# Column means of an 8192 x 8192 matrix: the last rows cut as 4, 4, 2 and 1 blocks, with five blocks loaded early and a small load behind the last

## The chip, the cores and the metric

The kernel runs on one core of one Trainium2 chip. The metric is the device time of one execution in microseconds; the median of three runs of the kernel before is 628.57 us (628.53 to 629.09). The profile covers a span of 626.7 us, from the first to the last instruction.

## The reference

```
x = randn(8192, 8192), float32          # 268.4 MB
out = mean(x, axis=0)                   # 8192 values, float32
```

All of `x` must be read once. A row group is 128 rows of `x`, one for each partition, so there are 64 groups (0 to 63) of 4 MB each. A block is F = 512 columns, so each group has 16 blocks.

## The kernel before

Loads run on SyncE's queue into four row buffers, two groups at a time. VectorE adds the two groups and then adds the sum to `acc`. The last groups come singly, and TensorE adds up what is left, with a matrix of `ones` filled with 1/8192 that also sums over the partitions. TensorE writes four blocks side by side, in four quarters of 32 partitions, which give one 512-column bank of PSUM. ScalarE and VectorE copy PSUM to SBUF, and from there the result is stored.

```python
load(head[:], rows(G - 4)[:, :3 * F])                   # 3 blocks of group 60, first of all
first, second = load_rows(0, 0, 4), load_rows(4, 4, 2)
load(ahead[:], rows(G - 1)[:, 8 * F:WHOLE * F])         # 4 blocks of group 63, early
...
while g < G - 10:                                       # groups 6 to 53, in pairs
    u = (g + 2) % 4
    dma = load_rows(g, u, 2)
    add(both, bufs[:, u, :], bufs[:, u + 1, :], [dma])
    add(acc, acc, both, [])
    g += 2
while g < G - 4:                                        # groups 54 to 59, singly
    row = bufs[:, (g + 2) % 4, :]
    add(acc, acc, row, [load(row, rows(g))])
    g += 1
for lo, loaded in [(3, 3), (5, 0)]:                     # groups 60 and 61
    row = bufs[:, (g + 2) % 4, :]
    dma = load(row[:, loaded * F:], rows(g)[:, loaded * F:])
    add(acc[:, lo * F:], acc[:, lo * F:], row[:, lo * F:], [dma])
    g += 1
...
load(r62, rows(g))                                      # group 62
tc.keep_in_program_order(nc.gpsimd.tensor_add(
    out=acc[:, 13 * F:], in0=acc[:, 13 * F:], in1=r62[:, 13 * F:]))
g += 1
for lo, hi in [(0, 8), (12, 14), (14, 16)]:             # group 63: the last three loads
    load(r63[:, lo * F:hi * F], rows(g)[:, lo * F:hi * F])
# ... matmuls, one for each block or half block, in the order of a plan:
#     ahead, acc, r61, head, acc, r62, acc, r63 0-8, r63 12-14, r63 14-16 ...
copy(res[:, 2, :], banks[2][:])                         # ScalarE
s2 = store(nc.scalar, <blocks 8-12>, res[0:P:32, 2, :], loads[-3])
for b in range(2):
    copy(res[:, b, :], banks[b][:])
copy(tails[0], ends[0][:])
nc.vector.tensor_copy(out=tails[1], in_=ends[1][:])
...
s01 = store(nc.sync, <blocks 0-8>, res[0:P:32, 0:2, :])
s3 = store(nc.scalar, <blocks 12-14>)
store(nc.sync, <blocks 14-16>)
```

The full source:

Of the kernel before, what the change touches and what calls it, by code (L numbers as in the profile page):

```python
# [8 lines left out]
@with_exitstack  # L9
def kernel(  # L10
    ctx: ExitStack,
    tc: tile.TileContext,
    x: bass.AP,
    out: bass.AP,
):

    nc = tc.nc
    f32 = mybir.dt.float32
    M, N = x.shape  # L40
    P = nc.NUM_PARTITIONS
    F = 512
    W = F // 2
    WHOLE = 12
    G = M // P
    U = 6
    sync = mybir.DependencyInfo(mybir.DependencyClass.Sync, mybir.DependencyReason.DATA)

    sb = ctx.enter_context(tc.tile_pool(name="sb", bufs=1))
    psp = ctx.enter_context(tc.tile_pool(name="psum", bufs=1, space=bass.MemoryType.PSUM))  # L50

    bufs = sb.tile([P, U, N], f32, name="bufs")
    both = bufs[:, U - 2, :]
    acc = bufs[:, U - 1, :]
    ones = sb.tile([P, 32], f32, name="ones")
    ahead = sb.tile([P, 4 * F], f32, name="ahead")
    tail = sb.tile([P, W], f32, name="tail")
    warm = sb.tile([P, 32], f32, name="warm")
    nc.gpsimd.memset(ones[:], 1.0 / M)  # L59
    ready = sb.tile([P, 1], f32, name="ready")  # L60
    tc.keep_in_program_order(
        nc.gpsimd.tensor_add(out=ready[:], in0=ones[:, 0:1], in1=ones[:, 1:2]))  # L62
    banks = [psp.tile([P, F], f32, name=f"bank{b}") for b in range(3)]
    ends = [psp.tile([P, W], f32, name=f"end{e}") for e in range(2)]

    loads = []

    def landed(*inss):

        nop = tc.keep_in_program_order(nc.sync.nop()).ins  # L70
        for o in inss:
            tc.add_manual_dep(nop, o.name, sync, reason="SyncE waits")

    def load(dst, src):
        ins = tc.keep_in_program_order(nc.sync.dma_start(out=dst, in_=src)).ins  # L75
        k = len(loads)
        over = loads[k - 8:k - 6] if k >= 8 and k % 2 == 0 else []
        tc.declare_no_dep(ins, group="loads", keep=over, reason="the reader of the buffer waited")
        for o in over:
            tc.add_manual_dep(ins, o.name, sync, reason="covers the next load too")  # L80
        tc.add_to_no_dep_group("loads", ins)
        loads.append(ins)
        return ins

    def rows(g, n=1):
        return x[g * P:(g + n) * P, :]

    def load_rows(g, u, n):
        return load(bufs[:, u:u + n, :], rows(g, n).rearrange("(p j) c -> p j c", j=n))

    adds, joins = [], {}

    def add(dst, a, b, dmas):

        ins = nc.vector.tensor_add(out=dst, in0=a, in1=b).ins  # L95
        if dmas and adds:
            waiter = nc.scalar if len(adds) % 8 > 1 else nc.gpsimd
            nop = joins[waiter] = tc.keep_in_program_order(waiter.nop()).ins  # L98
            for o in dmas + adds[-1:]:
                tc.add_manual_dep(nop, o.name, sync, reason="the no-op waits")  # L100
            for group in ("loads", "adds"):
                tc.declare_no_dep(ins, group=group, reason="the no-op waited")
            tc.add_manual_dep(ins, nop.name, sync, reason="waits for both at once")
        elif adds:
            tc.declare_no_dep(ins, group="loads", reason="the add ahead waited")
        tc.add_to_no_dep_group("adds", ins)
        adds.append(ins)

    head = sb.tile([P, 3 * F], f32, name="head")
    load(head[:], rows(G - 4)[:, :3 * F])  # L110
    first, second = load_rows(0, 0, 4), load_rows(4, 4, 2)
    load(ahead[:], rows(G - 1)[:, 8 * F:WHOLE * F])
    add(bufs[:, 2:4, :], bufs[:, 2:4, :], bufs[:, 0:2, :], [first])
    add(bufs[:, 4:6, :], bufs[:, 4:6, :], bufs[:, 2:4, :], [second])
    add(acc, acc, both, [])
    tc.keep_in_program_order(nc.scalar.copy(out=warm[:], in_=ones[:]))  # L116
    g = 6
    while g < G - 10:
        u = (g + 2) % 4
        dma = load_rows(g, u, 2)  # L120
        add(both, bufs[:, u, :], bufs[:, u + 1, :], [dma])
        add(acc, acc, both, [])
        g += 2

    while g < G - 4:
        row = bufs[:, (g + 2) % 4, :]
        add(acc, acc, row, [load(row, rows(g))])
        g += 1
    for lo, loaded in [(3, 3), (5, 0)]:
        row = bufs[:, (g + 2) % 4, :]  # L130
        dma = load(row[:, loaded * F:], rows(g)[:, loaded * F:])
        add(acc[:, lo * F:], acc[:, lo * F:], row[:, lo * F:], [dma])
        g += 1
    r61, r62, r63 = [bufs[:, (g + 1 + j) % 4, :] for j in range(3)]
    load(r62, rows(g))
    tc.keep_in_program_order(nc.gpsimd.tensor_add(  # L136
        out=acc[:, 13 * F:], in0=acc[:, 13 * F:], in1=r62[:, 13 * F:]))
    g += 1
    for lo, hi in [(0, 8), (12, 14), (14, 16)]:
        load(r63[:, lo * F:hi * F], rows(g)[:, lo * F:hi * F])  # L140

    plan = [
        (ahead, 8, 12),
        (acc, 3, 5),
        (acc, 0, 3),
        (r61, 0, 5),
        (head, 0, 3),
        (acc, 5, 12),
        (r62, 0, 12),
        (r62, 12, 13),  # L150
        (acc, 12, 14),
        (acc, 14, 16),
        (r63, 0, 8),
        (r63, 12, 14),
        (r63, 14, 16),
    ]
    sums = []
    for row, lo, hi in plan:
        base = 8 * F if row is ahead else 0
        if lo < WHOLE:  # L160
            for i in range(lo, hi):
                cols = row[:, i * F - base:(i + 1) * F - base]
                sums.append((banks[i // 4], i % 4, cols))
        else:
            for c in range(lo * F, hi * F, W):
                e, q = divmod(c // W - 2 * WHOLE, 4)
                sums.append((ends[e], q, row[:, c:c + W]))
    for n, (dst, q, cols) in enumerate(sums):
        tc.keep_in_program_order(nc.tensor.matmul(  # L169
            out=dst[32 * q:32 * q + 32, :],  # L170
            lhsT=ones[:],
            rhs=cols,
            start=all(d is not dst or k != q for d, k, _ in sums[:n]),
            stop=all(d is not dst or k != q for d, k, _ in sums[n + 1:]),
            tile_position=(0, 32 * q),
            skip_group_check=True,
        ))

    res = both[:, :3 * F].rearrange("p (b c) -> p b c", b=3)
    tails = [both[:, 3 * F:3 * F + W], tail[:]]  # L180

    def copy(dst, src):
        tc.keep_in_program_order(nc.scalar.copy(out=dst, in_=src))  # L183

    def store(engine, dst, src, *then):
        ins = tc.keep_in_program_order(engine.dma_start(out=dst, in_=src)).ins
        for o in then:
            tc.add_manual_dep(ins, o.name, sync, reason="follows that load")
        return ins

    def end(e):
        return (out[(WHOLE + 2 * e) * F:(WHOLE + 2 * e + 2) * F].rearrange("(q c) -> q c", q=4),
                tails[e][0:P:32, :])

    copy(res[:, 2, :], banks[2][:])
    s2 = store(nc.scalar, out[8 * F:12 * F].rearrange("(q c) -> q c", q=4), res[0:P:32, 2, :],
               loads[-3])
    for b in range(2):
        copy(res[:, b, :], banks[b][:])
    copy(tails[0], ends[0][:])  # L200
    nc.vector.tensor_copy(out=tails[1], in_=ends[1][:])  # L201
    landed(*loads[-8:-6])
    landed(*loads[-6:-4])
    landed(*loads[-4:-2])
    landed(*joins.values())
    s01 = store(nc.sync, out[:8 * F].rearrange("(b q c) -> q b c", b=2, q=4), res[0:P:32, 0:2, :])
    s3 = store(nc.scalar, *end(0))
    store(nc.sync, *end(1))
    landed(loads[-2], s2)
    landed(loads[-1], adds[-1])  # L210
    landed(s01, s3)
    hold = tc.keep_in_program_order(nc.vector.nop()).ins
    tc.add_manual_dep(hold, s01.name, sync, reason="VectorE ends late")


# [28 lines left out]
```

## Time and profile before

| what | value |
|---|---|
| time, median of 3 | 628.57 us |
| span of the profile | 626.7 us |
| VectorE busy | 526.1 us (84%), 60 instructions |
| TensorE, ScalarE, GpSimd busy | 17.6, 3.5 and 4.0 us |
| load queue, share of 16 engines | 99.2% |
| mean rate over the span | 428 GB/s |

The page's forty slices give the busy share of each engine in tenths, and below it that of the 16 transfer engines (DMA). The chain of waits goes back from the last instruction to what released it, and so tells which work the end hung on. The timeline lists instructions by start time, with the idle time ahead of them and what ended it in brackets. A "q" behind an engine's name is its queue of transfer issues; an issue takes some 0.3 to 1.1 us there, and the transfer itself lands later. Group 62 lands near 615.6 us, where GpSimd's add starts.

### The profile page before, as it was taken

To read this page: it belongs to the slowest core of one execution; us is meant where nothing else is said; L and a number is where in the kernel's file an instruction comes from. 1 tells how busy PE (TensorE), PEld (TensorE's weight loads), DVE (VectorE), ACT (ScalarE), POOL (GpSimd) and SP (SyncE) were. 2 spreads that over 40 slices of the span, in tenths; PEclk is the share of its full clock that TensorE was granted. 3 is DMA by queue.
4 is the path that set the end of the run, shared out by engine and by line. 5 is a ranking of instruction groups with operands and counts; after the bars stand their busy time and mean duration, and the time that the engine had idled before them with its cause. 6 is when DMAs were issued, how large, how long until landed. Compare 5 with 4: busy or idle time off the path is not lost.

```text
span 626.7 us, 475 instructions
## 1 busy us (share of the span) xinstructions
PE 17.6 (3%) x124; PEld 5.1 (1%) x124; DVE 526.1 (84%) x60; ACT 3.5 (1%) x6; POOL 4.0 (1%) x7
## 2 busy tenths in 40 slices
PE   0000100000000000000000000000000000000027
PEld 0000000000000000000000000000000000000002
DVE  0028999999888998888988889888898888999991
ACT  0000000000000000000000000000000000000001
POOL 0000000000000000000000000000000000000002
PEclk9999999999999999999999999999999999999999
DMA  9999999999999999999999999999999999999997
GB/s 385 468 402 409 461 443 427 410 460 406 464 402 468 402 468 402 468 402 468 402 468 402 468 402 468 402 460 410 443 427 414 456 402 435 435 435 435 420 433 305
DMA packets 5926, 268.50 MB, mean 428 GB/s; under 512 B 656, under 2 KB 664, under 8 KB 1060
## 3 DMA queue, kind: packets, MB, share of 16 engines
q1 hardware_dynamic: 5908, 268.46, 99.2%
q8 instruction: 1, 0.02, 0.0%
q10 hardware_dynamic: 16, 0.01, 0.0%
q14 instruction: 1, 0.01, 0.0%
HBM read 268.44 MB, written 0.03 MB: 428 GB/s over the span
## 4 chain that ended last, share of the span: by engine, by line
DMA 56%; DVE 33%; another core or an unknown queue 10%; issue 0%; SPq 0%; PE 0%; ACTq 0%; POOLq 0%; POOL 0%
DMA bufs<-in_x_dram 56%; DVE bufs L95 33%; SPq L75 0%; PE end L169 0%; ACTq L98 0%; DVE tail L201 0%; POOLq L98 0%; POOL ready L62 0%; POOL ones L59 0%; POOLq L228 0%
## 5 line engine op out<-in xcount | busy, mean ns | idle before, releaser
L95 DVE TENSOR_TENSOR bufs<-bufs 128x8192 f32<-128x8192 f32 (+3 forms) x59 | 525.6, 8909 | 87.9 <-DMA bufs<-in_x_dram 43.8
L169 PE MATMUL bank<-bufs,ones 128*32 128x512 f32 x74 | 12.8, 709 | 540.4 <-DVE bufs L95 539.9
L201 DVE COPY tail<-end 128x256 f32<-128x256 f32 x1 | 0.4, 425 | 10.2 <-PE end L169 10.2
L169 PEld LDWEIGHTS bank<-bufs,ones 128*32 128x32 f32 x74 | 3.2, 120 | 549.5 <-DVE bufs L95 541.6
L136 POOL TENSOR_TENSOR bufs<-bufs 128x1536 f32<-128x1536 f32 x1 | 3.5, 3469 | 614.6 <-DMA bufs<-in_x_dram 614.6
L183 ACT COPY bufs<-bank 128x512 f32<-128x512 f32 x3 | 1.8, 586 | 619.2 <-PE bank L169 616.6
L169 PE MATMUL bank<-ahead,ones 128*32 128x512 f32 x8 | 1.9, 1058 | 65.7 <-DMA ahead<-in_x_dram 65.7
L169 PE MATMUL end<-bufs,ones 128*32 128x256 f32 x36 | 3.3, 384 | 0.1
L169 PE MATMUL bank<-head,ones 128*32 128x512 f32 x6 | 1.9, 600 | 0.0
L169 PEld LDWEIGHTS end<-bufs,ones 128*32 128x32 f32 x36 | 1.4, 109 | 2.4 <-DMA bufs<-in_x_dram 0.9
L116 ACT ACT_TABLE_LOAD x1 | 1.3, 1283 | 0.7 <-PEq L228 0.7
L169 PEld LDWEIGHTS bank<-ahead,ones 128*32 128x32 f32 x8 | 0.2, 140 | 65.6 <-issue 65.6
L183 ACT COPY bufs<-end 128x256 f32<-128x256 f32 x1 | 0.4, 378 | 0.0
L169 PEld LDWEIGHTS bank<-head,ones 128*32 128x32 f32 x6 | 0.4, 108 | 0.6 <-issue 0.6
L116 ACT COPY warm<-ones 128x32 f32<-128x32 f32 x1 | 0.2, 218 | 0.0
L62 POOL TENSOR_TENSOR ready<-ones 128x1 f32<-128x1 f32 x1 | 0.2, 193 | 0.1
L59 POOL MEMSET ones<- 128x32 f32 x1 | 0.1, 125 | 0.3 <-POOLq L228 0.3
L228 POOL MEMSET const-bfloat16-1.0<- 128x1 bf16 x1 | 0.1, 101 | 0.0
L228 POOL MEMSET const-uint8-127<- 128x1 uint8 x1 | 0.1, 101 | 0.0
L228 POOL MEMSET const-float32-0.0<- 128x1 f32 x1 | 0.1, 99 | 0.2 <-issue 0.2
L228 POOL MEMSET const-float32-1.0<- 128x1 f32 x1 | 0.1, 99 | 0.0
## 6 DMA issues: line engine op xcount, KB each, us to landing
bufs<-in_x_dram SPq DMA_DIRECT2D x8, 4096.0 KB, 24.1
bufs<-in_x_dram SPq DMA_DIRECT2D x1, 3328.0 KB
bufs<-in_x_dram SPq DMA_DIRECT2D x1, 2048.0 KB, 20.2
ahead<-in_x_dram SPq DMA_DIRECT2D x1, 1024.0 KB
bufs<-in_x_dram SPq DMA_DIRECT2D x2, 512.0 KB, 21.5
head<-in_x_dram SPq DMA_DIRECT2D x1, 768.0 KB
bufs<-in_x_dram SPq DMA_DIRECT2D x26, 29.9
out_dram<-bufs ACTq DMA_DIRECT2D x1, 8.0 KB
```

The costliest lines, as they stand in the source:

```text
L59: nc.gpsimd.memset(ones[:], 1.0 / M)
L62: nc.gpsimd.tensor_add(out=ready[:], in0=ones[:, 0:1], in1=ones[:, 1:2]))
L95: ins = nc.vector.tensor_add(out=dst, in0=a, in1=b).ins
L116: tc.keep_in_program_order(nc.scalar.copy(out=warm[:], in_=ones[:]))
L136: tc.keep_in_program_order(nc.gpsimd.tensor_add(out=acc[:, 13 * F:], in0=acc[:, 13 * F:], in1=r62[:, 13 * F:]))
L169: tc.keep_in_program_order(nc.tensor.matmul(out=dst[32 * q:32 * q + 32, :], lhsT=ones[:], rhs=cols, start=all(d is not dst or k != q for d ...
L183: tc.keep_in_program_order(nc.scalar.copy(out=dst, in_=src))
L201: nc.vector.tensor_copy(out=tails[1], in_=ends[1][:])
L228: nc = _bacc.Bacc("TRN2", target_bir_lowering=False, num_devices=1)
```

## The change

The last group is cut so that the load that lands last is one block (256 KB) instead of two. Five of its blocks (9 to 14, the end not counted) are loaded early instead of four. They and two blocks of group 60 (14 and 15, in place of blocks 0 to 2) go to one tile, `early`, and GpSimd adds them to `acc` in mid-stream, behind groups 24 and 32, where before TensorE summed `ahead` and `head`. The other blocks of group 63 come last, as 4, 4, 2 and 1 blocks. The result goes out in five stores: blocks 9 to 14 first, then 4 to 8, 0 to 4, 14 to 16, and block 8 alone. In each of these ranges the four quarters of PSUM hold a quarter of the range each. Behind the last load, an unused one of 64 bytes a row (`trail`) is put in the same queue.

```diff
-    W = F // 2
-    WHOLE = 12
+    W = F // 4
...
-    load(head[:], rows(G - 4)[:, :3 * F])
+    load(early[:, 5 * F:], rows(G - 4)[:, 14 * F:])
     first, second = load_rows(0, 0, 4), load_rows(4, 4, 2)
-    load(ahead[:], rows(G - 1)[:, 8 * F:WHOLE * F])
+    load(early[:, :5 * F], rows(G - 1)[:, 9 * F:14 * F])
...
-        add(acc, acc, both, [])
+        add(acc, acc, both, ahead)
+        ahead = []
+        if g in (24, 32):
+            lo, hi = (0, 4) if g == 24 else (4, 7)
+            cols = slice((9 + lo) * F, (9 + hi) * F)
+            ins = tc.keep_in_program_order(nc.gpsimd.tensor_add(
+                out=acc[:, cols], in0=acc[:, cols], in1=early[:, lo * F:hi * F])).ins
+            tc.add_to_no_dep_group("early", ins)
+            ahead = [ins]
...
-    for lo, loaded in [(3, 3), (5, 0)]:
+    for lo, hi, loaded in [(0, 14, 14), (5, 16, 16)]:
...
-    tc.keep_in_program_order(nc.gpsimd.tensor_add(
-        out=acc[:, 13 * F:], in0=acc[:, 13 * F:], in1=r62[:, 13 * F:]))
+    for cols in [slice(14 * F, 16 * F), slice(8 * F, 9 * F)]:
+        tc.keep_in_program_order(nc.gpsimd.tensor_add(
+            out=acc[:, cols], in0=acc[:, cols], in1=r62[:, cols]))
     g += 1
-    for lo, hi in [(0, 8), (12, 14), (14, 16)]:
+    for lo, hi in [(4, 8), (0, 4), (14, 16), (8, 9)]:
         load(r63[:, lo * F:hi * F], rows(g)[:, lo * F:hi * F])
+    load(trail[:], rows(g)[:, :16])
...
+    blocks(acc, 2, 5)
+    blocks(acc, 0, 2)
+    blocks(r61, 0, 5)
+    blocks(acc, 5, 8)
+    spread(wide, acc, 9, 14)
+    blocks(r62, 0, 8)
+    spread(wide, r62, 9, 14)
+    blocks(r63, 4, 8)
+    spread(two, acc, 14, 16)
+    blocks(r63, 0, 4)
+    spread(last, acc, 8, 9)
+    spread(two, r63, 14, 16)
+    spread(last, r63, 8, 9)
...
+    copy(res5, wide[:, :5 * W])
+    s5 = store(nc.scalar, part(9, 14), res5[0:P:32, :], loads[-5])
+    copy(res[:, 1, :], banks[1][:])
+    copy(res[:, 0, :], banks[0][:])
+    copy(res2, two[:])
+    nc.vector.tensor_copy(out=tail[:], in_=last[:])
...
+    s1 = store(nc.sync, part(4, 8), res[0:P:32, 1, :])
+    s0 = store(nc.sync, part(0, 4), res[0:P:32, 0, :])
+    s2 = store(nc.scalar, part(14, 16), res2[0:P:32, :])
+    store(nc.sync, part(8, 9), tail[0:P:32, :])
```

## The prediction, made before the changed kernel had run

> **What bounds the kernel now.** I read the busy shares first, then the forty slices, then the chain of waits for the last 90 us, then the timeline of the last 4 us.
>
> The page: the DMA row stands at 9 in 39 of 40 slices, and VectorE, the busiest engine, is at 84%.
>
> ```profile
> PE 17.6 (3%) x124; PEld 5.1 (1%) x124; DVE 526.1 (84%) x60; ACT 3.5 (1%) x6; POOL 4.0 (1%) x7
> ...
> DMA  9999999999999999999999999999999999999997
> ...
> HBM read 268.44 MB, written 0.03 MB: 428 GB/s over the span
> ```
>
> The reader is to see that the kernel is one load stream: 268.44 MB must come in, and the transfer engines never pause. The packet records of the trace say the same: the first load's packets start at 1.7 us, the last one's end at 622.5 us. So the time is the start (1.7), the stream (about 620.8), and whatever follows the last byte. The change leaves the bytes alone; only their order and cutting differ.
>
> The end of the chain of waits (start us, us, what):
>
> ```profile
> 582.72 8.70 DVE bufs L95
> ...
> 591.52 8.70 DVE bufs L95
> 600.22 0.02 issue
> 600.24 0.33 SPq L75
> ...
> 601.09 21.93 DMA bufs<-in_x_dram
> 623.02 0.04 issue
> 623.06 0.68 PE end L169 x8
> 623.75 0.03 issue
> 623.77 0.42 DVE tail L201
> ```
>
> The VectorE pieces are only how the loads of the last rows were released: the last three were issued by 601.4 us and the very last landed at 623.0 us, so more than 20 us of other loads stood ahead of it. What counts is below: 8 matmuls (0.68 us), the copy out of PSUM (0.42 us), then the last store. From the timeline of the last 4 us:
>
> ```profile
> 622.58 0.59 ACT L183 COPY bufs<-bank 128x512 f32<-128x512 f32 x1 [0.27 <-PE bank L169]
> 623.07 0.38 ACT L183 COPY bufs<-end 128x256 f32<-128x256 f32 x1
> 623.20 0.70 SPq L186 DMA_DIRECT2D out_dram<-bufs  x1
> 623.48 0.52 ACTq L186 DMA_DIRECT2D out_dram<-bufs  x1
> 623.77 0.42 DVE L201 COPY tail<-end 128x256 f32<-128x256 f32 x1 [10.23 <-PE end L169]
> 624.22 0.56 SPq L186 DMA_DIRECT2D out_dram<-tail  x1
> ```
>
> The last store is issued at 624.22 us. In the landing records it lands at 625.87 (1.65 us after its issue began), the one from ScalarE's queue at 625.35 and SyncE's large one at 625.17; the closing instructions take the rest to 626.71. So the tail store is last, by 0.5 us. The measured 628.57 us is 1.86 us more than the span; I keep that.
>
> [...] the next-to-last load, which has a follower, has its first semaphore packet at 620.94 and its first landing at 621.50 (0.56 us); the last load, with none, 622.22 and 622.76 (0.54 us). Having a follower changed nothing.
> [...] rows of 16,384 bytes start every 612 ns, rows of 4,096 every 157 to 159 ns, where a quarter of 612 is 153: about 5 ns a row.
> [...] groups of 512-column matmuls take 0.86 us from 607.47 and 0.43 us from about 613 on.
>
> **The change part by part.**
> *Cutting of the stream.* Each transfer engine takes 8 rows of every load. From the spacings seen (6,144 bytes 231 ns, 16,384 612, 4,096 158) and about 27 bytes per ns plus 5 ns for the others, the loads that differ are, per 8 rows, before: 231 + 307 + 989 + 612 + 158 + 158 = 2,455 ns; after (4,096, 10,240, 28,672, 8,192 twice, 4,096, 2,048 bytes): 158 + 382 + 1,065 + 307 + 307 + 158 + 82 = 2,459 ns. Eight times 4 ns is 0.03 us; one more semaphore packet makes it about **+0.05 us**.
> *Two GpSimd adds in mid-stream.* The old one of 1,536 columns took 3.47 us, so 2,048 take about 4.6 us. They start where VectorE would idle 1.94 us (the timeline of the middle shows 17.42 us of adds in each 19.36). [...] VectorE regains 1.9 us a pair, and the next load is issued some 10 us before the stream needs it. **0**.
> *Tail, up to the last load.* VectorE's add on row group 60 grows from 6,656 to 7,168 columns, +0.5 us; its last add ends near 614.1 instead of 613.54, still before group 62 lands at 615.6. GpSimd's adds there remain 3.47 us in sum. PE loses the head block's matmuls, so it idles near 611 to 614[...]. The four landings come near 618.1, 620.6, 621.9 and 623.1; each has over 0.6 us behind it, against 0.43 or 0.86 for four 512-column matmuls. Hidden.
> *Store of the five blocks.* The old third-bank store kept ScalarE's queue 1.07 us from 620.57. The new one can go at about 619 and ends near 620.5. Its four rows of 2,560 bytes share four of the engines with the loads in flight, about 0.1 us each; two of those had spare time before (semaphore packets from 622.22 to 622.53). I book **+0.07 us** for the last landing. It comes at about 623.1 to 623.2.
> *Last matmuls.* One matmul of 256 columns has a latency of 0.38 us, its second set of four starts 0.21 us after the first: together 0.68. Four of 128 columns: 0.38 - 0.11 = 0.27, plus start 0.07: 0.35. **-0.33 us**[...].
> *Copy.* 256 columns took 425 ns; at VectorE's pace in the adds (8,192 columns in 8.70 us) 128 fewer are 136 ns fewer: **-0.14 us**.
> *Last store.* Rows of 512 bytes instead of 1,024 took 44 ns per packet: **-0.02 us**. It is the last on SyncE's queue; the stores of the two banks, split in two, go at about 621.2 and 621.9, before it. ScalarE's last store comes from the 14-to-16 load landing near 622.45: matmuls 0.35 to 0.5, copy 0.38, so about 623.3, against 623.48 before, and lands before the tail store.
> *The unused load.* 8 rows of 64 bytes per engine[...]. It delays stores that are not last, and by the landing records it doesn't hasten the load ahead. **0**.
>
> Sum: 0.05 + 0.07 - 0.33 - 0.14 - 0.02 = **-0.37 us**: a span near 626.3, a time near 628.2 us.
>
> **The rivals.**
> (a) *A bound from ScalarE's queue.* If the early store is slow to be taken while three loads are still queued (the old one already took 1.07 us, its like at the end 0.52), the copies of both banks and the 14-to-16 blocks slip behind it, SyncE's bank store slips, and the tail store queues behind that one. For it: ScalarE is strictly in order, and waited 2.59 us behind that store before. Against it: about 2 us of room. It would give 628.5 to 628.9.
> (b) *The small load shortens the last landing*[...]. For it: nobody adds an unused load without having seen something. Against it: 0.56 against 0.54 us above. If true by 0.2 us: 628.0.
> (c) *It costs*: one more transfer in front of the stores, and its landing is awaited at the end. It must land before 625.5, which is 2.4 us later: no effect unless the stores become late.
> (d) *The gain drowns.* Three runs of before range from 628.53 to 629.09, more than the gain.
>
> **Range and chances.** The sum of small terms has an uncertainty of some 0.2 us ([...]early store +0.1, (b) -0.2), the measurement about as much again: 627.7 to 628.8. 2% is 12.6 us, and no part comes near it, short of the stream stalling over the GpSimd adds. So within 2%: 0.99.
>
> **What would show it.** Last load landing at 623.1 to 623.2 in the trace after; four PE matmuls of about 0.35 us; a VectorE copy near 0.29; the tail store issued near 623.8 and last to land; DMA at 9 throughout; one VectorE add held by 2 to 3 us in mid-stream. Wrong would be: a bank store still occupying SyncE after 623.8, the last landing over 0.2 us away from 623.1, or a gap in the stream.

## The result, and the profile after

The changed kernel takes 630.68 us, median of 5 (630.48 to 630.88), against 628.59 (628.53 to 629.09) for the kernel before on the same chip: a ratio of 1.0032, 95% interval 1.002 to 1.0044. That is 2.5 us above the predicted 628.2 and outside its range of 627.7 to 628.8.

First the page of the changed kernel: the forty slices of the transfer engines, and the transfer queues with packets, MB and share of the 16 engines.

```profile
DMA  9999999999999999999999999999999999999995
...
q8 instruction: 1, 0.02, 0.0%
...
q14 instruction: 1, 0.01, 0.0%
HBM read 268.44 MB, written 0.03 MB: 427 GB/s over the span
```

The stream is still without a gap; only the last slice fell from 7 to 5, so the time was lost at the end. The two "instruction" lines stand in the page of before as well. The prediction read past them: one packet of 16,384 bytes (q8) and one of 8,192 (q14), which the page calls instruction traffic. By the packet times below they run on the same transfer engines as the data.

The end of the chain of waits (start us, us, what):

```profile
601.57 22.97 DMA bufs<-in_x_dram
624.54 0.04 issue
624.58 0.47 PE last L183 x8
...
625.08 0.29 DVE tail L214
```

The last load lands at 624.54, not at 623.1 to 623.2. Behind it all is as predicted: a short set of matmuls and a copy of 0.29 us. The timeline shows what TensorE waited for (in brackets: idle time, and what ended it), and when the tail store was issued:

```profile
624.58 0.42 PE L183 MATMUL last<-bufs,ones 128*32 128x128 f32 x8 [1.40 <-DMA bufs<-in_x_dram]
625.08 0.29 DVE L214 COPY tail<-last 128x128 f32<-128x128 f32 x1 [10.99 <-PE last L183]
625.39 0.50 SPq L201 DMA_DIRECT2D out_dram<-tail  x1
```

One line of SyncE's own waits (us in total, times, longest):

```profile
SPq L254 <- DMA out_dram<-tail: 1.4, 1, 1.4
```

The wait for the tail store is 1.4 us long here. The same line of before:

```profile
SPq L239 <- DMA out_dram<-tail: 0.2, 1, 0.2
```

The packet records tell why. They carry no engine numbers; the packets of one engine are told apart by following one another without a gap. Each load lands as 16 semaphore writes in these records, which are read as one for each of the 16 transfer engines. Fifteen of the last load's came by 623.136, as predicted. On the sixteenth engine the 16,384-byte packet ran from 622.356 to 623.456, between the last load's rows and its semaphore packet, which started at 623.442, and that write came at 624.540. In before the same packet ran on one engine from 622.359 to 623.437, but all 16 writes of the last load were in by 623.020: the packet came *behind* the semaphore packet of its engine (the nearest one starts 6 ns ahead of it), and so delayed nothing. The two moments differ by 3 ns; what differs is which side of the last semaphore write the packet takes.

The balance of the span, 626.711 before and 628.898 after (landings from the landing records, the rest from the instruction records):

```
                                              before     after    difference
last load landed                              623.020   624.540   +1.520
from there to VectorE's copy                    0.751     0.537   -0.214
copy                                            0.425     0.291   -0.134
tail store: issue to its normal landing         1.643     1.575   -0.068
one of its four landings later than the rest    none      0.835   +0.835
last landing to the end                         0.845     1.093   +0.248
```

The fourth row runs from the issue of the tail store to its landing (in after, of three of its four parts); between the copy's end and this issue lie another 0.027 us in both. The fifth is a second packet: the 8,192-byte one ran from 626.460 to 626.767 on an engine that carried a quarter of the tail store, whose row went out at 626.763, and landed at 627.805 against 626.97 for the other three. In before that packet starts at 626.331, after everything had landed. The sixth is a closing instruction of SyncE: it took 120 ns, and started 0.38 us behind its like on ScalarE (628.570 and 628.195). In e1 below, the same one takes 7 ns and starts 5 ns ahead of ScalarE's.

So three terms cost 2.60 us, and the gains that the prediction counted on are there, 0.42 us in sum.

### The profile page after: what moved, and what is told of

Read it like the earlier page. It is cut to its first block, busy times and chain, and to the rows that moved or that the text cites. A ratio compares the mean times of both kernels' runs of the same rounds, so it can differ in the third digit from the quotient of the medians.

```text
span 628.9 us, 481 instructions
## 1 busy us (share of the span) xinstructions
PE 14.8 (2%) x122; PEld 4.4 (1%) x122; DVE 530.4 (84%) x60; ACT 3.7 (1%) x6; POOL 12.0 (2%) x10
## 4 chain that ended last, share of the span: by engine, by line
DMA 55%; DVE 34%; another core or an unknown queue 10%; issue 0%; SPq 0%; ACTq 0%; PE 0%; POOL 0%; POOLq 0%
DMA bufs<-in_x_dram 55%; DVE bufs L97 34%; SPq L77 0%; ACTq L100 0%; PE last L183 0%; POOLq L100 0%; DVE tail L214 0%; POOL ready L62 0%; POOL ones L59 0%; POOLq L243 0%
## 5 line engine op out<-in xcount | busy, mean ns | idle before, releaser
L183 PE MATMUL bank<-bufs,ones 128*32 128x512 f32 x58 | 11.2, 742 | 608.8 <-DVE bufs L97 608.1
L130 POOL TENSOR_TENSOR bufs<-bufs,early 128x2048 f32<-128x2048 f32 (+1 forms) x2 | 7.9, 3954 | 348.4 <-DVE bufs L97 348.4
L149 POOL TENSOR_TENSOR bufs<-bufs 128x1024 f32<-128x1024 f32 (+1 forms) x2 | 3.6, 1832 | 259.0 <-DMA bufs<-in_x_dram 259.0
L183 PE MATMUL wide<-bufs,ones 128*32 128x512 f32 (+1 forms) x32 | 3.4, 433 | 0.0
L183 PEld LDWEIGHTS wide<-bufs,ones 128*32 128x32 f32 x32 | 1.3, 110 | 2.3 <-issue 2.3
L183 PE MATMUL two<-bufs,ones 128*32 128x256 f32 x16 | 1.3, 385 | 0.0
```

Of the source, the lines that this page charges most:

```text
L130: ins = tc.keep_in_program_order(nc.gpsimd.tensor_add(out=acc[:, cols], in0=acc[:, cols], in1=early[:, lo * F:hi * F])).ins
L149: tc.keep_in_program_order(nc.gpsimd.tensor_add(out=acc[:, cols], in0=acc[:, cols], in1=r62[:, cols]))
L183: tc.keep_in_program_order(nc.tensor.matmul(out=dst[32 * q:32 * q + 32, c:c + cols.shape[1]], lhsT=ones[:], rhs=cols, start=all((d is dst, ...
```

## The experiments

The diffs show the lines that matter, without the indices that follow from them. The letters in the expectations: by A the small load is to blame; by B it is not, and the new cutting brings the packet in ahead of the last landing. By P the 16,384-byte packet is TensorE's next piece of program, so that its moment goes with the matmuls; by Q the early bank stores let it in; by S the shape of the last loads does. R and T are rivals of P and Q: the packet does not go with the matmuls, or something other than the stores lets it in. In the text of e8 alone, V and S say that the 8,192-byte packet follows VectorE or ScalarE. All of these were guesses of the author, which no trace had shown. "Landing" is the last of the 16 writes of the last load. Several kernels show two groups of times; then both are given. In all runs of the kernel before, none is above 629.35.

**The small load alone (e1, e2, e3).** e1 is the changed kernel without it; e2 the kernel before with it, behind its last load; e3 the changed kernel with it one place earlier.

```diff
-    load(trail[:], rows(g)[:, :16])                       # e1
```
```diff
+    load(trail[:], rows(g)[:, :16])                       # e2, in the kernel before
```
```diff
-    for lo, hi in [(4, 8), (0, 4), (14, 16), (8, 9)]:     # e3
+    for lo, hi in [(4, 8), (0, 4), (14, 16)]:
         load(...)
     load(trail[:], rows(g)[:, :16])
+    load(r63[:, 8 * F:9 * F], rows(g)[:, 8 * F:9 * F])
```

> The changed kernel without the small unused load behind the last one; all else stays. In the changed kernel one transfer engine carries a 16 KB instruction packet from 622.36 to 623.46 us, between the last data packet of the last load and its semaphore packet, so that load lands at 624.54 instead of about 623.14. Theory A (the small load is to blame[...]): the instruction packet comes behind the last semaphore, the last landing is near 623.1, and the time is 628.1 to 628.5. Theory B (the collision comes from the time at which the instruction packet is asked for, and the small load is a bystander): 630.3 to 630.9, last landing near 624.5.

> The kernel before, with the same small unused load of 64 bytes a row put behind its last load, and waited for at the end. Theory A: the instruction packet, which in the kernel before starts 6 ns behind the last semaphore packet of its engine, now gets in ahead of a semaphore packet that the end waits for; 629.5 to 631. Theory B: the engine's last load semaphore is out by 622.353 as before, only the small load behind is held up; 628.5 to 629.0, at most a few tenths more because its landing (about 624.7) is awaited, which is before the last store lands.

> The changed kernel with the small unused load moved from behind the last load to just ahead of it. Number of loads, instructions and bytes stay. Theory A: nothing stands behind the last load, so the last landing is near 623.2 and the time 628.1 to 628.6. Theory B: the last load still ends some 0.1 us after the moment at which the instruction packet comes, so it is still held, 630.3 to 631.

e1: 630.21 us, ratio 1.0017 (1.0004 to 1.003); five executions at 630.13 to 630.78 and two at 628.0 and 628.31. e2: 628.61, ratio 1.0 (0.9991 to 1.0009). e3: 630.55, ratio 1.0033 (1.0019 to 1.0046). The end of e1's chain:

```profile
601.58 22.87 DMA bufs<-in_x_dram
...
624.49 0.47 PE last L181 x8
...
624.99 0.29 DVE tail L212
```

The late landing is there without the small load, and in e2 the small load makes no difference: it is not what delays the last load. Without it the closing instruction of SyncE takes its 7 ns again. And two of e1's seven executions take the time that the prediction had given the change, which none of the changed kernel's five did; with so few executions that may be chance, and e12 below has the small load and both groups of times.

**Fewer and more matmuls (e4, e5, e6).** These change TensorE's program alone. e4 leaves out 5 of the 61 matmuls (row group 61, columns 0 to 2,559), e5 thirteen (also row group 62, blocks 0 to 7); so their sums lack those parts of `x`. e6 is the kernel before with 12 small matmuls ahead of all others, whose result is not used.

```diff
-    blocks(r61, 0, 5)          # e4 and e5
-    blocks(r62, 0, 8)          # e5 only
```
```diff
+    for _ in range(12):        # e6, in the kernel before, ahead of the matmuls
+        nc.tensor.matmul(out=spare[0:32, :], lhsT=ones[:], rhs=ones[:], ...)
```

> The changed kernel with TensorE's five matmuls over row group 61 left out (20 instructions of TensorE's stream; columns 0 to 2559 of the output then miss group 61). If the 16 KB instruction packet is TensorE's own next stretch of program, asked for at a fixed place of its stream, it is asked for 20 instructions later or not at all: then the last load lands near 623.1 and the time is 628.0 to 628.6. If the packet has nothing to do with TensorE's instruction count, it comes near 622.36 again and the time stays at 630.3 to 630.9.

> The changed kernel with 13 matmuls of TensorE left out (row group 61's five blocks and row group 62's eight: 52 instructions of TensorE; the output then misses those parts). Leaving out five gave two clusters, 628.6 to 629.5 and 630.1 to 630.5. Theory P (the 16 KB instruction packet is TensorE's next stretch of program, asked for at a fixed place of its stream; in the changed kernel that place is reached shortly before the last load has ended): 52 instructions later lies behind the last load's landing or is never reached, so no packet is seen before 622.7, the last landing is near 623.1 and every run is in one cluster, 627.9 to 628.5. Rival R (the packet has another requester and comes near 622.4 whatever TensorE does): two clusters or 630.3 to 630.8 again.

> The kernel before with 12 additional small matmuls at the very start of TensorE's stream (48 instructions; they write to a PSUM tile that nothing reads, and run in the first microseconds). Theory P: the instruction packet is asked for 48 instructions earlier in the tail, which TensorE reaches at 615 to 619 us; the packet is seen there instead of at 622.36, its engine loses 0.6 to 1.1 us of its stream, and the last load lands at 623.6 to 624.1 instead of 623.02: 629.1 to 629.9. Rival R: the packet stays at 622.36 and the time at 628.6.

e4: nine executions at 628.64 to 629.5 and eleven at 630.06 to 630.48 (median 630.09, ratio 1.0017, 1.001 to 1.0024); the profiled one is of the lower group, its packet follows the semaphore packet, and the load lands at 623.188. e5: 628.77 (628.54 to 629.89), ratio 1.0003 (0.9995 to 1.0012). Its page has no q8 line at all; the load lands at 622.964 and the tail store at 625.388. e6: 629.86, ratio 1.0019 (1.0011 to 1.0026), though its added work lies at the very start of the program. In its trace the packet comes at 619.665, 2.7 us sooner than in before, between the last row of the eight-block load on its engine and that load's semaphore packet, with two more loads to follow. The engine that took it stays behind: the last load lands at 624.157 instead of 623.020. The chain shows where it hit:

```profile
600.27 21.55 DMA bufs<-in_x_dram
...
621.96 1.92 PE bank L174 x16
623.88 1.00 PE end L174 x16
```

TensorE could start the sixteen matmuls of the eight-block load only at 621.96, and the last ones queued behind them. So a packet alone makes the kernel before 1.2 us slower, with its loads, adds and stores untouched.

**Other ways to move the packets (e7, e8).** e7 computes the whole mean without the small load: VectorE adds blocks 8 to 15 of row group 62, in three instructions more, in place of eight matmuls and GpSimd's two adds; VectorE's closing no-op is held as in e8. e8 is the changed kernel with VectorE's closing no-op held until a later store, to move the 8,192-byte packet, which starts 1.13 to 1.17 us behind VectorE's closing branch in before and in e2 to e6 (1.37 in the changed kernel).

```diff
-    for cols in [slice(14 * F, 16 * F), slice(8 * F, 9 * F)]:                       # e7
-        nc.gpsimd.tensor_add(out=acc[:, cols], in0=acc[:, cols], in1=r62[:, cols])
+    for cols in [slice(9 * F, 14 * F), slice(14 * F, 16 * F), slice(8 * F, 9 * F)]:
+        add(acc[:, cols], acc[:, cols], r62[:, cols], dmas, kept=True)              # VectorE
```
```diff
-    tc.add_manual_dep(hold, s0.name, ...)                                           # e8
+    tc.add_manual_dep(hold, s2.name, ...)
```

> A whole computation with fewer matmuls. From the changed kernel: no small load behind the last one; VectorE instead of GpSimd and TensorE adds blocks 8 to 15 of row group 62 to the accumulator (2,560, 1,024 and 512 columns, about 2.7, 1.2 and 0.7 us from 616.3), which saves TensorE 8 matmuls (32 instructions); and VectorE's closing no-op waits for the store of blocks 14 and 15 instead of that of blocks 0 to 3. Theory P: the packet comes behind the last load or never, last landing near 623.1, tail store issued near 623.8: 627.9 to 628.4, and below the kernel before. Rival R: last landing near 624.5 in most runs, 629.3 to 630.6.

> The changed kernel, but VectorE's closing no-op waits for the landing of the store of blocks 14 and 15 (625.27 us) instead of that of blocks 0 to 3 (624.67). In the changed kernel one quarter of the last store lands at 627.81, 0.84 us behind the other three (626.97), on an engine that carries an 8 KB instruction packet from 626.46 to 626.77. In the runs so far such a packet followed VectorE's closing branch by 1.13 to 1.38 us and ScalarE's last instruction by 1.55 to 1.76 us. Theory V (it follows VectorE): it comes at about 627.0, the last store lands at about 627.0, and the time is 629.7 to 630.1. Rival S (it follows ScalarE): it stays near 626.4 and the time at 630.5 to 630.8. The first collision, that of the last load, stays under both.

Both missed. e7: 629.92, ratio 1.002 (1.0013 to 1.0028). Its 16,384-byte packet came at 623.065 and did no harm, but an 8,192-byte one came at 485.608 in mid-stream (VectorE's program is three instructions longer; that this brought it is not shown), and from there on one engine lagged: the 16 landings of one load spread over 1.16 us (568.300 to 569.465), where in e18 the same load's spread over 0.43 (568.552 to 568.978), and the last load landed at 623.715. With the late landings the chain ends on ScalarE. e8: 630.90, ratio 1.0034 (1.0021 to 1.0047). VectorE's branch moved, from 625.091 to 625.456, and the packet followed at 626.591; but the tail store, late because of the last load (landing 624.687), still met it and landed at 628.161. Moving one packet did not help while the other still came in.

**Fewer matmuls with nothing left out (e9, e10, e11).** e9 has no small load, four blocks early (9 to 12), late loads of 4, 4, 3 and 1 blocks, and so 53 matmuls. e10 is e9 with the small load; e11 is e9 with 8 idle matmuls at the start, which bring TensorE's count back to 61.

```diff
-    for lo, hi in [(4, 8), (0, 4), (14, 16), (8, 9)]:    # e9
+    for lo, hi in [(4, 8), (0, 4), (13, 16), (8, 9)]:
-    spread(wide, acc, 9, 14)                             # and all that goes with it
+    spread(wide, acc, 9, 13)
```

> A whole computation built on what the runs showed. From the changed kernel: no small load; four blocks of the last group loaded early (9 to 12) instead of five, the late loads are 4, 4, 3 and 1 blocks; the four blocks need no splitting, so TensorE has 53 matmuls instead of 61 (32 instructions fewer); VectorE's instructions as before; SyncE's list has 81 instructions instead of 82. Theory P: the 16 KB packet comes behind the last landing (about 623.1), the last store is issued near 623.8 and lands near 625.4 with nothing in its way, and SyncE's closing step takes 7 ns as in the kernels with up to 81 instructions: 627.9 to 628.3, below the kernel before by some 0.4 us. Rival: something else than the packet makes the changed kernel's stream or end longer, 628.7 or more.

> The same with the small unused load behind the last one put back (83 instructions on SyncE). If the small load costs only its own issue and the room in SyncE's list: in all kernels with 82 instructions SyncE's closing step took 106 to 120 ns and came some 0.25 us late, so +0.2 to +0.3 us, 628.1 to 628.6. If it shields the last load in some way, as it may have been meant to: 627.6 to 627.9. If it is to blame for the collision: 629.5 or more.

> The kernel with 53 matmuls and no small load, plus 8 small matmuls of 32 columns at the very start of TensorE's stream, whose result nothing reads (32 instructions, done in the first microseconds). Nothing else changes. Theory P: the 16 KB packet is asked for 32 instructions earlier, as in the changed kernel, and collides with the last load again: last landing near 624.4, 629.9 to 630.6 in most runs. Rival (the number of TensorE's instructions is irrelevant): as without them, within 0.1 us.

e9: 628.55 (628.4 to 629.99, ten of thirteen at or below 628.77), ratio 1.0002 (0.9994 to 1.001). e10: 628.97 in two groups, seven at 628.53 to 628.97 and six at 629.45 to 630.02, ratio 1.0009 (1.0 to 1.0017). e11: 628.58, nine at or below 628.84 and three near 629.5, ratio 1.0003 (0.9995 to 1.0012). In all three profiles the packet (622.12, 622.163, 622.576) follows the last load's rows. e9 took the late times from most executions, but e11 is a clear miss: eight matmuls more did not bring them back, as theory P in its plain form (the count decides) would have it. And e9 gains nothing over before, as its last matmuls come behind those of the three-block load:

```profile
600.38 21.98 DMA bufs<-in_x_dram
...
622.40 0.85 PE three L182 x8
623.25 0.26 PE last L182 x8
```

**The bank stores (e12, e13, e14).** e12 is the changed kernel with its two bank stores as one, e13 that without the small load, e14 the changed kernel with its bank stores held until the last load has landed.

```diff
-    s1 = store(nc.sync, part(4, 8), res[0:P:32, 1, :])    # e12, e13
-    s0 = store(nc.sync, part(0, 4), res[0:P:32, 0, :])
+    s01 = store(nc.sync, out[:8 * F]..., res[0:P:32, 0:2, :])
```
```diff
+    landed(loads[-2])                                     # e14, ahead of s1
     s1 = store(nc.sync, part(4, 8), res[0:P:32, 1, :])
```

> The changed kernel with the stores of blocks 0 to 3 and 4 to 7 made one again, as before the change; it can then be issued only when the second bank has been copied, near 623.0, instead of from 621.86 on. Theory Q (the issue of a bank store on SyncE's queue, while that queue's last load is still running, is what lets the waiting 16 KB instruction packet in ahead of the rest of the load: in the four collisions seen the packet came 0.39 to 0.52 us after that issue began, at 622.36, 622.28, 622.44 and 622.46, and where no such issue fell into the last load it came 3 to 9 ns after its engine's loads had run out): the packet comes behind the last load, which lands near 623.1; SyncE's list is at 79 instructions; 628.0 to 628.5. Rival T (the shape of the last loads or the moment of the request decides): 630.0 to 630.8 as in the changed kernel.

> The same without the small unused load. Theory Q: 627.9 to 628.3, the time that the prediction's sum gave for the cut of the last loads alone, and below the kernel before. Rival T: two clusters near 628.2 and 630.3, as without the small load alone.

> The changed kernel with two bank stores as it has them, but the first of them waits for the last load's landing (SyncE waits there). This keeps the number of stores and moves only the time of their issue. Theory Q: no collision, last landing near 623.1; both bank stores and then the tail store stand in line on SyncE, 0.66, 0.51 and 0.50 us, so the tail store is issued near 624.45 and lands near 626.0; with SyncE's late closing step 628.6 to 629.2. Rival T: last landing near 624.5, 631 or more.

e12: 630.15, five executions at 628.12 to 628.74 and eight at 630.13 to 630.84, ratio 1.0017 (1.0008 to 1.0026); in the profiled one of the upper group the packet runs from 622.490, 0.6 us *before* SyncE issues the store at 623.115, and the load lands at 624.670. e13: 630.38, two at 628.55 and 628.71 and eight at 630.07 to 630.71, ratio 1.0023 (1.0014 to 1.0032). e14: 630.40, two at 629.18 and 629.35 and ten at 630.29 to 630.68, ratio 1.0028 (1.0019 to 1.0036). Theory Q falls. The profiled execution of e14 is the one at 629.18. Its packet comes at 622.329, behind the load's rows and semaphore packet, and the load lands at 623.162:

```profile
600.71 20.53 DMA bufs<-in_x_dram
...
621.28 1.07 PE bank L183 x8
...
622.57 0.64 PE two L183 x8
...
623.21 0.47 PE last L183 x8
```

Here the chain runs back through TensorE to the four-block load: the last load was there before TensorE was. TensorE's last matmuls start 1.37 us sooner than in the changed kernel, whose packet came ahead of the semaphore write; the two kernels differ besides only in when the bank stores are issued.

**The shape of the last loads (e15, e16).** e15 is e1 with 8, 2 and 1 blocks in place of 4, 4, 2 and 1, and with four matmuls over blocks 14 and 15 of `acc` moved ahead of the eight-block load's; e16 the kernel before with 4, 4, 2 and 2 in place of 8, 2 and 2.

```diff
-    for lo, hi in [(4, 8), (0, 4), (14, 16), (8, 9)]:    # e15
+    for lo, hi in [(0, 8), (14, 16), (8, 9)]:
```
```diff
-    for lo, hi in [(0, 8), (12, 14), (14, 16)]:          # e16, in the kernel before
+    for lo, hi in [(0, 4), (4, 8), (12, 14), (14, 16)]:
```

> The changed kernel without its small load, with its late loads cut 8, 2 and 1 blocks in place of 4, 4, 2 and 1; the matmuls and everything else stay. Theory S (the shape and number of the last loads decides whether the 16,384-byte packet lands ahead of the last load): the packet follows the last load's data, the last landing is near 623.2 and the time is 628.0 to 628.5 in nearly all executions, 0.1 to 0.6 us under the kernel before. Rival (the packet follows the matmuls' number and their moment, whatever the loads): part of the executions at 628.2 and part near 630.3, as without the small load.

> The kernel before with its late load of eight blocks cut in two, so that the late loads are 4, 4, 2 and 2 blocks; the matmuls, adds and stores stay. Theory S: the 16,384-byte packet gets in ahead of the last load in a part of the executions, which then take 629.5 to 630.5. Rival: 628.6 in all of them, as before, since the matmuls are the same.

e15: 629.03, all thirteen at 628.75 to 629.19, ratio 1.0008 (0.9999 to 1.0016). e16: 628.6 (628.42 to 629.02), ratio 1.0001 (0.9992 to 1.0009). Half of S holds: in e15 the upper group is gone and the load lands at 622.988. Half falls: four loads do not bring it in in the kernel before. Nor does e15 gain, as the matmuls of the eight-block load are now what the last ones wait behind:

```profile
600.18 20.88 DMA bufs<-in_x_dram
...
621.20 1.92 PE bank L181 x16
623.12 0.22 PE last L181 x8
...
623.77 0.25 PE last L181 x8
```

**Without the packet (e17, e18).** e18 is e1 without the thirteen matmuls of e5, so its sum lacks the same parts of `x`; loads, adds, copies and stores are those of the changed kernel. e17 leaves nothing out: it is e9 with VectorE adding the first five blocks of row group 61 in its last add, which leaves 48 matmuls as well.

```diff
-    blocks(r61, 0, 5)                                         # e17 and e18
-    blocks(r62, 0, 8)                                         # e18 only
-    for lo, hi, loaded in [(0, 14, 14), (5, 16, 16)]:         # e17 only
+    for lo, hi, loaded in [(0, 14, 14), (0, 16, 16)]:
```

> The whole computation with 48 matmuls: the kernel of e9 (no small load, four blocks of the last row group early, late loads of 4, 4, 3 and 1 blocks), with VectorE adding the first five blocks of row group 61 in its last add in place of five matmuls; that add then ends near 616.8 us and the matmuls of columns 0 to 4,095 start there. Theory P (the 16,384-byte packet is TensorE's next block of program): there is no such packet, the last landing is near 623.0, and no execution lies in a cluster above 629.4. If the matmuls keep up the time is 628.3 to 628.6; if they start too late[...], the last ones follow the landing by up to 0.8 us and it is 628.6 to 629.2. Rival (the packet comes whatever TensorE runs, and with 48 matmuls it was missing by chance): a packet of 16,384 bytes is in the trace.

> The changed kernel without its small load and without 13 matmuls (row group 61 columns 0 to 2,559 and row group 62 blocks 0 to 7 are left out of the sum); all loads, adds, copies and stores as in the changed kernel. If the packet is the cause of the two groups of times without the small load (628.0 to 628.3 and 630.1 to 630.8) and the closing stall of 0.25 us belongs to the small load's kernels, this one takes 628.0 to 628.5 in all executions, which is where the prediction's sum had put the change. If something other than the packet holds the last landing, executions near 630.3 remain.

e18: 628.45; twelve of thirteen executions at 628.03 to 628.63, one at 629.56, ratio 0.9998 (0.999 to 1.0007). Its page has the queues q1, q10 and q14 and no q8:

```profile
q1 hardware_dynamic: 6056, 268.46, 99.3%
q10 hardware_dynamic: 16, 0.01, 0.0%
q14 instruction: 1, 0.01, 0.0%
```

The load lands at 623.261 and the tail store at 625.722. With the same four loads, stores and copies as e1, and no packet of 16,384 bytes, the group at 630 is gone, as it was in e5, which has the small load. e17: 632.13 (631.5 to 632.79), ratio 1.0056 (1.0044 to 1.0069). It missed on both counts. Its chain:

```profile
616.18 3.65 PE bank L181 x16
619.83 1.71 PE wide L181 x8
621.54 1.98 PE bank L181 x16
```

TensorE starts only when VectorE's add ends, takes 3.65 us for sixteen matmuls that take 1.92 in e15, and never catches up. And its page does have a q8 packet, at 626.208, though TensorE runs 48 matmuls as in e5 and e18, where there was none. So the number of matmuls does not settle whether the packet comes either.

## Why the prediction was wrong, point by point

**What bounds the kernel** was right: one load stream without a gap, then what follows the last byte. (The third of the last loads was issued by 601.52, not 601.4, which changes nothing.)

**Cutting of the stream, +0.05, and the last landing at 623.1 to 623.2.** Right for fifteen of sixteen engines: 623.136 against 623.020 is +0.12, the booked 0.05 + 0.07. The step that failed is the last landing: its path held the loads and one store, and no instruction packet. Booked as +0.12 in all, it measured +1.52 (624.540), since the sixteenth engine carried the 16,384-byte packet ahead of its semaphore write. That the packet's place is the cause rests on the trace, where the one engine that is late, by 1.40 us, is the one with the packet; on e5 and e18, where without the packet the upper group of times is gone; and on e14, where with the packet behind the load it lands at 623.162. No program was profiled in both of its groups: the profiled executions of e4, e13 and e14 are of the lower group and have the packet behind, those of e1 and e12 are of the upper and have it ahead. A last landing "over 0.2 us away from 623.1" is what the prediction itself had named as proof against it.

**The GpSimd adds in mid-stream, 0.** Right. The two timelines:

```profile
276.58 4.49 POOL L130 TENSOR_TENSOR bufs<-bufs,early 128x2048 f32<-128x2048 f32 x1 [275.45 <-DVE bufs L97]
```
```profile
278.43 37.48 DVE L97 TENSOR_TENSOR bufs<-bufs 128x8192 f32<-128x8192 f32 x4 [1.93 <-ACTq L100]
317.15 17.42 DVE L97 TENSOR_TENSOR bufs<-bufs 128x8192 f32<-128x8192 f32 x2 [1.24 <-ACTq L100]
```

GpSimd took 4.49 us (4.6 predicted). Four VectorE adds took 37.48 us, where twice the 17.42 of an ordinary pair is 34.84: they took 2.64 us longer (2 to 3 predicted), and for 2.64 us, from 278.43 to 281.07, the first of them ran beside the GpSimd add. The second GpSimd add took 3.42 us and ran for 1.56 us beside a VectorE pair, which took 18.87 us, 1.45 longer. That an add would be held was the author's assumption: in the kernel before no GpSimd add of some length runs beside a VectorE add (its one of 3.47 us starts at 615.74, VectorE's last ends at 613.54). The next idle time is 1.24 instead of 1.93, and no load came late.

**Tail, up to the last load: hidden.** Only just. VectorE's last add ended at 614.08 (614.1 predicted), but the first three of the last loads landed at 618.72, 621.21 and 622.50, each 0.6 later than predicted, and TensorE was not idle near 611 to 614: it ran without a gap from 608.10. The matmuls of blocks 14 and 15 ended at 623.18 (622.54 and 0.64 us), 0.04 behind the landing of the other fifteen engines. Had the last load come in time, they would have been in its way, as they are in e18 below.

**Last matmuls -0.33, copy -0.14, last store -0.02.** Right in sign, and the copy in size: landing to copy -0.21, copy -0.13, the store's way to its normal landing -0.07. The matmuls gained two thirds of their term: the eight take 0.47 us in the chain where the prediction had 0.35, so 0.21 less than the 0.68 of before, and not 0.33.

**Tail store lands last, near 625.4; nothing behind it.** The order was right, the time not. It was issued at 625.39 instead of 623.8 because of the load, and there met the 8,192-byte packet: +0.84. In e1, e3, e8 and e12 too one part of the tail store lands later than the rest, by 0.56 to 1.08 us. The closing steps took +0.25, which no term had. In the traces of after, e3, e4, e5, e8 and e14, whose SyncE program has 82 instructions (counted as in the expectations; one fewer in the trace), the closing instruction comes late, in after 0.47 us behind the step ahead of it and in before 0.09. In e10, with 83, that instruction is on time but the step ahead of it is late, 0.47 us behind its own forerunner (0.15 in before), and the time from the last landing to the end is as long, 1.10 us. In e7, e9, e11 and e17, with 81, the step behind is late by 0.05 to 0.07. So the pause keeps to a place in SyncE's program and not to one instruction; what makes it was not tried by itself.

**The unused load, 0.** Right for the last landing, which is as late without it (e1: the last matmuls start at 624.49) and in the kernel before is no sooner with it (e2: 623.134, in a chain whose last wait for data starts at 601.18; before: 623.020 and 601.09). At the end it is not 0: SyncE's closing instruction took 120 ns with it and 7 ns without (e1), and came 0.38 us behind ScalarE's with it and 5 ns ahead without.

**The rivals.** (a) did not happen: the early store left ScalarE in time, and the bank stores left SyncE by 623.5. (b) did not happen: e2's last landing is 623.134, not sooner. (c) in the form given did not happen. (d) describes e9 and e18, whose intervals include 1. No rival named the packet.

**Where the predicted gain is.** The two lower times of e1, 628.0 and 628.31, lie about the predicted 628.2. But e18, without the packet, has a median of only 0.10 us under before (628.45 and 628.55), where the sum had 0.37. Its profile is 0.14 us shorter than that of before, and tells where the rest is:

```profile
622.68 0.64 PE two L179 x8
623.32 0.46 PE last L179 x8
...
623.80 0.29 DVE tail L210
```

The last load lands at 623.261, +0.24 where the sum had +0.12, and from there to the copy it takes 0.21 us less than in before, not 0.33: the last matmuls start as those of blocks 14 and 15 end. The other terms hold. No variant is reliably faster than the kernel before.

**What stays open** is what decides the packet's place. Ruled out as the sole cause: the small load (e1), the early bank stores (e12 to e14), the number of matmuls (e11, e17), four late loads (e16). What the traces do show is where it gets in. In the changed kernel, e8 and e12 no row of the last load was left on that engine ahead of its semaphore packet, nor any row of its load in e6; in e1 and e3 two rows were left, and two in e7 at the 8,192-byte packet in mid-stream. So in four of these seven cases an engine turned to the packet between the last row of a load and its own semaphore write, and in three with two of its 8 rows still to come. What makes an engine turn to it there is not shown. Small differences in the packet's moment may decide, as two groups of times from one program suggest; that is the author's guess. The kernel before shows no second group: in none of its 185 executions here did it take more than 629.35 us. In its profile all 16 writes of the last load were in by 623.020, with the packet behind; in the changed kernel the packet ahead cost 1.40 us at the last landing (624.540 against 623.136). Whose program it is stays open too: e6, where TensorE's alone was changed, moved it by 2.7 us, and e17 speaks against the plain count of matmuls.

## What to carry to other kernels

Before a change of tenths of a microsecond at the end of a stream, look in the queue part of the page for "instruction" lines and in the packet records for the moment of those packets. Here they ran on the same transfer engines as the data, and the last load was as late as its latest engine: fifteen had written by 623.136, TensorE started at 624.58, behind the sixteenth at 624.540. Which side of the last semaphore write the packet took was worth 1.40 us there, and an edit far away could change its place: the kernel before kept its time through e2 and e16 (628.61 and 628.6 us), and lost 1.2 us to twelve idle matmuls (e6). Take 10 executions or more, and look for two groups before the median is believed. Look too at whether the matmuls of the piece before the last are done when the last one lands: in e15 and e18 it landed at 622.988 and 623.261, but its matmuls started at 623.77 and 623.32, when those of the piece before had ended (e9: 623.25), and no gain beyond the intervals was left.

## What the runs showed of the hardware that was not expected

- The 16,384-byte instruction packet held one transfer engine for 1.02 to 1.11 us in these runs, where a row of the same size took 612 ns. Two rows of 2,048 bytes behind it took 445 ns in e1, where two took 164 otherwise. In the changed kernel the semaphore packet behind it landed 1.10 us after its start, where the last load of before took 0.54.
- An engine that lost time in mid-stream had not got it back 83 us later: in e7, with a packet at 485.608, the landings of one load spread over 1.16 us (568.300 to 569.465), against 0.43 for the same load in e18.
- The cost went with the packet's place: in the changed kernel 1.40 us for 16,384 bytes ahead of the last semaphore write and 0.84 us for 8,192 bytes beside a store of 512-byte rows; in before nothing for 16,384 bytes just behind its engine's semaphore packet (all 16 writes in by 623.020).
- Twelve idle matmuls at the start of a program, some 600 us away from its end, made the end 1.2 us later (e6: a span of 627.9 us against 626.7).
